# Expert weights in 8 KB rows: 128x2048 words a load, nineteen places, four column groups of one bank

## The chip, the cores and the metric

One Trainium2 chip, one of its cores. The metric is the device time of one execution in microseconds, as the median of several runs; a profile of one execution tells where that time goes. TensorE multiplies matrices into PSUM banks, VectorE (DVE), ScalarE (ACT) and GpSimd (POOL) work on tiles in SBUF and on those banks, and SyncE (SP) issues most DMAs. Sixteen DMA engines share the core's transfers.

## What is computed

The reference runs two blocks on one sequence of 256 tokens with 1024 features, all in float32. The first block has two layers of attention and a feed-forward net; the second has one token mixer (long convolution, a recurrence with states from a context) and a mixture of experts. The change is about that last part:

```python
def expert_choice_moe(h, p):
    cap = EC_CAPACITY * T // N_EXPERTS                  # 32 tokens an expert, 16 experts
    affinity = jax.nn.softmax((h @ p['router_w']).astype(jnp.float32), axis=-1)
    gates, idx = lax.top_k(jnp.swapaxes(affinity, 1, 2), cap)
    xe = jax.vmap(lambda hb, ib: hb[ib])(h, idx)
    hid = jax.nn.silu(jnp.einsum('becd,edf->becf', xe, p['exp_w1'])) * jnp.einsum('becd,edf->becf', xe, p['exp_w3'])
    ye = jnp.einsum('becf,efd->becd', hid, p['exp_w2']) * gates[..., None].astype(h.dtype)
    return jax.vmap(lambda ib, yb: jnp.zeros((T, D), yb.dtype).at[ib.reshape(-1)].add(yb.reshape(-1, D)))(idx, ye)
```

exp_w1 and exp_w3 are 1024 x 2048 for each expert and exp_w2 is 2048 x 1024: 24 MB of weights an expert, 16 of them.

## The kernel before

**Weights.** All weights but the experts' come through `Stream` (L64) in the order of their use, in loads of 1 MB into four tiles `wraw0` to `wraw3`, all on SyncE's queue. `pump_splits` (L94) splits pieces of 128x1024 words into two float32r parts: ACT casts into a tile `whi` (L113), DVE subtracts into a tile `wlo` (L114); there are three of each, and three pieces are split ahead. TensorE multiplies with both parts (`mm3`, L343). In most of these loads a row, which is what lies contiguously for one partition, is 1 or 2 KB long; the chunks of `modulation` (L371, from ada_w and mod_w) and the load of x into `xT` have rows of 8 KB, and the first eight of those chunks come in halves with rows of 4 KB.

**Slots.** Activations live in 26 equal tiles of 128x1024 words (`slot`, L311), three more from `tokens` (L1643) on. `drop` (L324) puts a slot at the end of the list of free ones and `slot` takes the first. A slot that is taken is a new tile of its tag, so its first writer waits for all users of the tile that had the tag before.

**The experts.** `Experts` (L149) lists the weights of the 16 experts in the order of their use as pieces of [128, 2, 512] words: 256 rows of 2 KB, 512 KB, 48 for each expert. Each goes into a room: at the start of `moe` (L1843) these are the free slots but five (`slot_rooms`, L1802), the halves of the stream's raw tiles and the six tiles whi and wlo (`stream_rooms`, L1812), then two halves of `xT` once its rows have been copied. `done` (L180) gives the room of the piece that was used last to the next load, or hands it back: the first five (`ex.back = 5`) become slots again. SyncE issues the loads (L1844) in this order; each waits for its room.

Before the first expert the router's product, the choice of 32 tokens for each expert and `pick` (L1897) must be done: one-hot products fetch the rows of four experts at a time into a tile `xe`, features on the partitions.

An expert then runs over four quarters `c` of its 2048 hidden features. For w1 and w3 it takes four pieces each; a piece holds two blocks of 128 input features, and block k0 + j is multiplied in column group (k0 + j) mod 4 of a bank, so a piece has two matmuls in two of the four groups of 32 columns. `part` (L1944) copies the bank, eight products with `i32` sum the four groups and turn them, ACT makes SiLU (L1952), DVE the product (L1953), and four pieces of w2 follow into two banks `py`. After the fourth quarter the sums `ye` (L1972) are multiplied with the gates and added to `acc` (L1991). After the last expert comes a norm, and four DMAs write the result (L2009).

The core of the inner loop:

```python
for k0 in range(0, 8, 2):
    w = ex.take()
    for j in range(2):
        q = 32 * (k0 % 4 + j)
        mm(p[q:q + 32, :], xe[e // 4][:, k0 + j, ee], w[:, j, :], start=k0 < 4, stop=k0 >= 4)
    ex.done()
```

All of TensorE's products are written on L340, so their tiles tell them apart: x<-s, x<-wraw and the like with 128x512 are w1 and w3, mm<-...,hid is w2, x<-i,part the turning. One float32 matmul is two instructions.

Of the kernel before, what the change touches and what calls it, by code (L numbers as in the profile page):

```python
# [27 lines left out]
NSLOT = 26  # L28
NLATE = 3
KEEP = 5  # L30
PICKS = ((0, 2), (1, 1), (2, 1))
SLOTW = 1024

# [5 lines left out]
class Slot:  # L39
    """A view of a slot's tile and the slot's tag."""  # L40

    def __init__(self, v, t, tag):
        self.v, self.t, self.tag = v, t, tag
# [5 lines left out]
class Halves:  # L49
    """Tiles that follow one another along the first free axis, `per` entries in each."""  # L50
# [13 lines left out]
class Stream:  # L64
    """The weights in the order of their use: chunks of 128 x 2048 words are loaded ahead. Pieces of a chunk are
    split ahead into two float32r parts whose sum is the weight, or stay as they are where the key is in `whole`; a
    chunk that comes with a function goes to it as it is, when the pieces before it have been taken."""
# [26 lines left out]
    def pump_splits(self):  # L94
        g = self.g
        nc = g.nc
        while self.split_pos < len(self.order) and self.split_pos < self.take_pos + self.ahead:
# [10 lines left out]
            hi = g.wsp.tile([128, 1024], FR, name="whi", tag="whi")  # L108
            lo = g.wsp.tile([128, 1024], FR, name="wlo", tag="wlo")
            hv = hi[:, :k * n].rearrange("p (k n) -> p k n", k=k)  # L110
            lv = lo[:, :k * n].rearrange("p (k n) -> p k n", k=k)
# [38 lines left out]
class Experts:  # L150
    """The experts' weights in the order of their use, [128, 2, 512] at a time, into whatever room there is."""

    def __init__(self, I, load):
        self.load = load
        self.aps = []
        for e in range(16):
            w1, w3, w2 = (I[n][0, e].rearrange("(k p) n -> p k n", p=128) for n in ("exp_w1_2", "exp_w3_2", "exp_w2_2"))
# [40 lines left out]
def constants():  # L198
# [7 lines left out]
    c["c_mask"] = np.ascontiguousarray(m.reshape(3, 2, 128, S).transpose(1, 2, 0, 3))  # L206

    # decay-ordered triangles within chunks of 64 tokens: rows s, columns t; per direction strict, inclusive
# [3 lines left out]
    # the implicit filter's features and decay window  # L212
# [8 lines left out]
    # real transforms over 512 points: cosines, sines (column 0: the alternating signs of the last frequency)  # L221
# [17 lines left out]
def vectors():  # L239
    """Vectors wanted one feature per partition: (name, input, its part, columns of 128)."""  # L240
# [12 lines left out]
def lay_out(inputs):  # L253
    """The inputs as the chip reads them: x and the context by features, the vectors side by side."""
# [38 lines left out]
def _build(g, I, out):  # L293
# [10 lines left out]
    more = []  # L304
    free_slots = [f"s{i}" for i in range(NSLOT)]

    def at(tag, shape, dt=FT):
        uid[0] += 1
        return (act if int(tag[1:]) < NSLOT else more[0]).tile(shape, dt, name=f"{tag}_{uid[0]}", tag=tag)

    def slot(name, shape, dt=FT):  # L311
# [4 lines left out]
        uid[0] += 1  # L316
        t = at(tag, [128, SLOTW], dt)
        v = t[:shape[0], :n]
# [3 lines left out]
        return Slot(v, t, tag)  # L322

    def drop(*ts):  # L324
        for t in ts:
            assert t.tag not in free_slots
            free_slots.append(t.tag)
# [3 lines left out]
    def wt(name, shape, dt=FT):  # L331
        """A short-lived tile, in the rotating slots of its size."""
# [19 lines left out]
    def by_tile(key, w, c0, c1):  # L352
        """Columns c0:c1 of a 1024-row matrix, out tile by out tile."""
# [17 lines left out]
    def modulation(m, i):  # L371
        """2048 columns of cond @ W, one feature per partition, into mods[m][:, 16 i:16 i + 16] (per vector)."""
# [35 lines left out]
    def among(main, asides):  # L408
        """The asides spread evenly over the main ones."""
# [62 lines left out]
    # vectors, one feature per partition  # L472
# [7 lines left out]
    # the first columns of the first layer's modulation, in slots  # L480
# [27 lines left out]
    # conditioning vectors, silu'd, as 32-column stationary operands with one (or two) live columns  # L508
# [17 lines left out]
    def reduce_angle(o, x, shape):  # L526
        """x less its nearest multiple of 2 pi."""
# [16 lines left out]
    def whole_gains(l):  # L544
        """The gains of the features that turn are in the tables."""
# [4 lines left out]
    def tables():  # L550
        """What the first layer's attention needs."""
# [33 lines left out]
        # lambda of both layers, on every partition  # L585
# [39 lines left out]
    def rsq(ss, scale, add):  # L625
        """(scale ss + add) ** -0.5 of a narrow tile."""
# [35 lines left out]
    def on_all(rs):  # L662
        """One number for each token, on every partition."""
# [7 lines left out]
    def rms_bcast(x):  # L671
        """(mean of squares over the features + eps) ** -0.5, on every partition."""
# [9 lines left out]
    def modulate(x, mul, add, exact=None, rs=None):  # L682
        """h = rms(x) * mul + add, split (and as it is)."""
# [22 lines left out]
    def wst(key, xh, xl, nk, tiles, finish, per=1, outer=False, bank="mm"):  # L706
        """Out tiles (128 features x 256 tokens), two to a bank; a piece holds `per` of them."""
# [26 lines left out]
    def alternate(gens):  # L734
        """Their steps in turn."""
# [8 lines left out]
    def staggered(gens, lag):  # L744
        """Their steps, each `lag` steps after the one before it; the later ones first."""
# [12 lines left out]
    def urgent(gen, n):  # L758
        """Its steps with a higher priority."""
# [11 lines left out]
    def layer(l):  # L771
# [85 lines left out]
        def attn_a(h, oh, ss, i0):  # L857
            """Head h: its output over the first component's sum of exponents, token by partition."""
# [45 lines left out]
        def heads_a(half):  # L904
# [3 lines left out]
            # the norm over a head's 128 features, features to the partitions  # L908
# [1123 lines left out]
```

## Time and profile before

| | us |
|---|---|
| median of 3 runs | 2614.85 |
| lowest, highest | 2611.32, 2617.59 |
| span of the profiled execution | 2612.7 |
| of it before the experts' steady transfers (0 to 1596) | 1596.0 |
| expert stage (1596 to 2598) | 1002.0 |
| end (2598 to 2612.7) | 14.7 |

For the profiled execution the span is the one time that is known; it lies 2.15 us under the median. In the profile PE is TensorE's matmuls and PEld its loads of stationary operands. The stretches are read from the views by windows and by time.

### The profile page before, as it was taken

The page shows a single profiled execution, that of the slowest core. Times are in us where ns is not written, and L with a number is a line of the kernel's source. Part 1 is how long each engine was busy: PE and PEld are TensorE (multiplying, and loading weights), DVE is VectorE, ACT ScalarE, POOL GpSimd, SP SyncE. Part 2 cuts the span into 40 slices and gives each one's busy share as a digit, 9 for nine tenths or more (in the row PEclk, how much of TensorE's full clock was granted, in tenths as well). Part 3 has the DMA queues.
Part 4 walks back from the last instruction along what each step waited for, and adds up shares of the span by engine and source line. Part 5 has one row for each costly group of instructions (what it writes and reads, how often), then busy time and mean ns, then how long its engine had stood idle before and what let it go on. Part 6 is the DMA issues. An engine that isn't in the chain of part 4 may idle for free. (4 is left out here: it accounts for less than half of the span.)

```text
span 2612.7 us, 39350 instructions
## 1 busy us (share of the span) xinstructions
PE 2364.9 (91%) x15946; PEld 1539.9 (59%) x15946; DVE 1179.6 (45%) x2239; ACT 833.8 (32%) x1539; POOL 114.0 (4%) x137
## 2 busy tenths in 40 slices
PE   7999999999999999998999888888888888888887
PEld 3678798898677777998987764332222222222222
DVE  5666577976667646667775552111111111111112
ACT  3654347545455423444562421110000000000001
POOL 0011000000011000000000010000000000000001
PEclk9999999999999998999999888899999999999999
DMA  9655554774655454655425376999999999999997
GB/s 352 217 181 193 171 180 167 226 244 156 244 190 197 158 189 133 200 181 170 145 84 158 98 246 213 386 386 387 386 387 387 387 386 386 386 386 386 384 386 284
DMA packets 386015, 678.35 MB, mean 260 GB/s; under 512 B 35208, under 2 KB 138153, under 8 KB 377514
## 3 DMA queue, kind: packets, MB, share of 16 engines
q1 hardware_dynamic: 384762, 671.64, 73.0%
q0 software_dynamic: 1072, 4.20, 0.4%
q8 instruction: 126, 2.06, 0.3%
q14 instruction: 55, 0.45, 0.0%
HBM read 671.31 MB, written 4.46 MB: 259 GB/s over the span
## 5 line engine op out<-in xcount | busy, mean ns | idle before, releaser
L340 PE MATMUL mm<-s,whi 128*128 128x256 f32 x3888 | 736.9, 289 | 12.0 <-DVE s L699 4.5
L340 PEld LDWEIGHTS mm<-s,whi 128*128 128x128 f32 x3888 | 614.8, 194 | 58.0 <-issue 33.2
L340 PE MATMUL mm<-s,wlo 128*128 128x256 f32 x1944 | 557.4, 287 | 2.2 <-DVE wlo L114 2.1
L340 PE MATMUL x<-s,s 128*32 128x512 f32 (+8 forms) x3276 | 462.7, 398 | 56.1 <-DMA s<-in_exp_w 51.8
L113 ACT CAST whi<-wraw 128x1024 fp32r<-128x1024 f32 x327 | 341.9, 1049 | 501.4 <-PE mm L340 408.0
L114 DVE TENSOR_TENSOR wlo<-wraw,whi 128x1024 fp32r<-128x1024 f32 x327 | 399.9, 1225 | 210.6 <-ACT whi L113 204.3
L340 PEld LDWEIGHTS mm<-s,wlo 128*128 128x128 f32 x1944 | 376.0, 194 | 14.0 <-issue 6.5
L1944 DVE COPY part<-x 128x512 f32<-128x512 f32 x64 | 44.3, 692 | 693.7 <-PE x L340 691.6
L340 PEld LDWEIGHTS x<-s,s 128*32 128x32 f32 (+5 forms) x3276 | 183.7, 141 | 287.4 <-DMA s<-in_exp_w 157.3
L340 PE MATMUL mm<-whi,s 128*128 128x512 f32 (+1 forms) x768 | 226.7, 373 | 2.1 <-ACT qn L818 1.5
L340 PEld LDWEIGHTS x<-i,part 128*128 128x128 f32 x1024 | 123.7, 191 | 149.6 <-DVE part L1944 92.6
L1944 ACT COPY part<-x 128x512 f32<-128x512 f32 x64 | 37.5, 585 | 460.4 <-PE x L340 460.4
L340 PE MATMUL x<-i,part 128*128 128x32 f32 x1024 | 137.1, 278 | 43.6 <-DVE part L1944 42.9
L340 PEld LDWEIGHTS mm<-whi,s 128*128 128x128 f32 x768 | 138.3, 190 | 40.2 <-issue 8.7
L340 PE MATMUL mm<-wlo,s 128*128 128x512 f32 (+1 forms) x384 | 143.7, 376 | 0.6 <-DVE wlo L114 0.6
L340 PE MATMUL mm<-s,hid 128*32 128x512 f32 x616 | 124.0, 739 | 21.0 <-DVE hid L1953 20.2
L1952 ACT ACTIVATE hid<-x 128x128 f32<-128x128 f32 x64 | 17.7, 277 | 389.9 <-PE x L340 389.9
L630 POOL TENSOR_TENSOR ry<-ru,nhalf 128x8 f32<-128x8 f32 (+4 forms) x47 | 73.0, 1555 | 865.1 <-DVE ru L629 648.9
L340 PE MATMUL x<-wraw,s 128*32 128x512 f32 x352 | 84.1, 616 | 13.0 <-DMA wraw<-in_exp_w 13.0
L340 PE MATMUL g<-wraw,cond 128*32 128x512 f32 x512 | 90.1, 621 | 4.2 <-DMA wraw<-in_ada_w 2.5
L340 PEld LDWEIGHTS mm<-wlo,s 128*128 128x128 f32 x384 | 73.0, 190 | 23.9 <-issue 4.1
L340 PEld LDWEIGHTS mm<-s,hid 128*32 128x32 f32 x616 | 27.0, 121 | 74.3 <-DVE hid L1953 25.8
(389 smaller groups left out, 2264.2 us busy)
## 6 DMA issues: line engine op xcount, KB each, us to landing
s<-in_exp_w SPq DMA_DIRECT2D x460, 512.0 KB, 10.8
wraw<-in_w_in SPq DMA_DIRECT2D x83, 1024.0 KB, 5.4
wraw<-in_exp_w SPq DMA_DIRECT2D x132, 512.0 KB, 10.8
wraw<-in_ada_w SPq DMA_DIRECT2D x40, 1024.0 KB, 5.0
whi<-in_exp_w SPq DMA_DIRECT2D x66, 512.0 KB, 10.8
wlo<-in_exp_w SPq DMA_DIRECT2D x66, 512.0 KB, 10.8
wraw<-in_w_mlp_up SPq DMA_DIRECT2D x32, 1024.0 KB, 5.5
wraw<-in_w_mlp_down SPq DMA_DIRECT2D x32, 1024.0 KB, 5.1
```

What stands on the lines that cost most here:

```text
L113: nc.scalar.copy(hv, src)
L114: nc.vector.tensor_sub(lv, src, hv.bitcast(FT))
L340: nc.tensor.matmul(*a, **k)
L630: nc.gpsimd.tensor_tensor(y, u, nhalf[:sh[0]].to_broadcast(sh), op=OP.pow)
L1944: (nc.vector.tensor_copy if i else nc.scalar.copy)(t, p)
L1952: nc.scalar.activation(hid, p[:, 0:128], AF.Silu)
```

## The change

- An expert's weights come in rows of 8 KB: 128x2048 words, 1 MB a load. For w1 and w3 a load is one block of 128 input features with all 2048 hidden ones; for w2 a row holds two neighbouring hidden features' 1024 words. There are 24 loads an expert, 384 in all.
- The places for them are 128x2048: `whi` and `wlo` become one tile `whl` of two halves, the raw tiles are used whole, `xT` is one place, and the slots become halves of 13 tiles (`Pair`), with one pair and one single tile more from `tokens` on. 12 pairs, 3 raw tiles, 3 `whl` and `xT` make nineteen places; two are handed back (`ex.back = 2`).
- `slot` takes the half that was freed longest ago, of a pair in use if no more than four pairs are wholly free (and of the same type of number), else of any. A pair that is wholly free begins a new tile. `gate` takes the newest (`newest=True`) where the list was turned round.
- `hidden` multiplies a load in four matmuls, one for each 512 hidden features, in the four column groups of one bank, over eight loads. Two such banks (w1, w3) are copied and turned by transposes with every second column, SiLU and product run over 512 columns, and the eight loads of w2 go into one bank `py`, 64 rows for each half of the features. The copy of `py`, the gates' products over 64 rows and the sums follow.
- `pick` runs after experts 0, 1 and 4; the fourth set of rows reuses the first's tile. The last norm's gains are made at the start of expert 15.
- The mask of the second attention is one tile of four parts and one DMA, not two tiles of three parts and two DMAs.

```diff
@@ Stream.pump_splits
-            hi = g.wsp.tile([128, 1024], FR, name="whi", tag="whi")
-            lo = g.wsp.tile([128, 1024], FR, name="wlo", tag="wlo")
+            hl = g.wsp.tile([128, 2, 1024], FR, name="whl", tag="whl")
+            hv, lv = (hl[:, j, :k * n].rearrange("p (k n) -> p k n", k=k) for j in range(2))
@@ Experts
-            for c in range(4):
-                self.aps += [w[:, k:k + 2, 512 * c:512 * c + 512] for w in (w1, w3) for k in range(0, 8, 2)]
-                self.aps += [w2[:, k:k + 2, a:a + 512] for k in (4 * c, 4 * c + 2) for a in (0, 512)]
+            for n in ("exp_w1_2", "exp_w3_2"):
+                w = I[n][0, e].rearrange("(k p) n -> k p n", p=128)
+                self.aps += [w[k] for k in range(8)]
+            w = I["exp_w2_2"][0, e].rearrange("(m p j) n -> m p (j n)", p=128, j=2)
+            self.aps += [w[m] for m in range(8)]
@@ slot
-        tag = free_slots.pop(0)
+        free = [(q.freed[h] if q.used else max(q.freed), i, h) for i, q in enumerate(pairs) for h in range(q.width)
+                if h not in q.used and (not q.used or q.dt == dt)]
+        halves = [f for f in free if pairs[f[1]].used]
+        _, i, h = (max if newest else min)(halves if halves and sum(not q.used for q in pairs) <= SPARE else free)
+        q = pairs[i]
+        if not q.used:
+            q.new(dt)
@@ layer
-        maskt = [slot("maskc", [128, 3, S]) for _ in range(2)]
-        for t in range(2):
-            nc.gpsimd.dma_start(maskt[t].v, I["c_mask"][t])
+        maskt = slot("maskc", [128, 4, S])
+        nc.gpsimd.dma_start(maskt.v, I["c_mask"])
@@ stream_rooms
-        return [half(t, i) for t in raw for i in range(2)] + [room("whi"), room("wlo")] * 3
+        return [room(g.wraw, r) for r in ws.rooms] + [room(g.wsp, "whl")] * 3
@@ moe
-        ex.more(slot_rooms(KEEP))
+        whole = sorted((q for q in pairs if q.width == 2), key=lambda q: max(q.freed))
+        ex.more(slot_rooms(whole[:-2]))
...
-        ex.back = 5
+        ex.back = 2
+        def hidden():
+            p = pst("mm")
+            for k in range(KT):
+                w = ex.take()
+                for c in range(4):
+                    mm(p[32 * c:32 * c + 32, :], x_[:, k, ee], w[:, 512 * c:512 * c + 512], start=k == 0, stop=k == KT - 1)
+                ex.done()
+            return p
...
+            for i, src in enumerate((pa, pb)):
+                t = wt("part", [128, 512])
+                (nc.vector.tensor_copy if i else nc.scalar.copy)(t, src)
+                p = pst("x")
+                for b in range(4):
+                    a = 256 * (b // 2) + b % 2
+                    nc.tensor.transpose(p[:, 128 * b:128 * b + 128], t[:, a:a + 255:2], ident)
+                hid.append(p)
+            h = wt("hid", [128, 512])
+            nc.scalar.activation(h, hid[0], AF.Silu)
+            nc.vector.tensor_tensor(h, h, hid[1], op=OP.mult)
+            py = pst("mm")
+            for m in range(8):
+                w = ex.take()
+                for j in range(2):
+                    a = 128 * (2 * (m % 2) + j) + 32 * (m // 2)
+                    for i in range(2):
+                        q = 64 * i + 32 * j
+                        mm(py[q:q + 32, :], h[:, a:a + 32], w[:, 1024 * j + 512 * i:1024 * j + 512 * i + 512],
+                           start=m == 0, stop=m == 7)
+                ex.done()
```

## Rows read from the trace of the kernel before

**Rows 1.** Page: DMA's busy tenths and rate in 40 slices of the span.

```profile
DMA  9655554774655454655425376999999999999997
GB/s 352 217 181 193 171 180 167 226 244 156 244 190 197 158 189 133 200 181 170 145 84 158 98 246 213 386 386 387 386 387 387 387 386 386 386 386 386 384 386 284
```

**Rows 2.** Chain of waits, 1300 to 2620 us: shares by line.

```profile
by line: DMA s<-in_exp_w 32.8%; PE x L340 17.0%; DMA wraw<-in_exp_w 11.5%; PE mm L340 7.6%; DMA whi<-in_exp_w 5.7%; DMA xT<-in_exp_w 4.2%; DVE part L1944 1.6%; issue 1.3%; DMA wlo<-in_exp_w 0.8%; DVE hid L1953 0.6%; ACT hid L1952 0.6%; POOL
```

**Rows 3.** Windows by stretch (first line names the columns).

```profile
core 0: us, PE busy (x) PEld busy (x) DVE busy (x) ACT busy (x) POOL busy (x), PEclk, DMA share, GB/s
0.00:1596.00 1596.00, 1523.44 (x11606) 1259.27 (x11607) 1050.09 (x1991) 750.60 (x1352) 107.19 (x131) 0.96 0.55 184
1596.00:2598.00 1002.00, 837.64 (x4336) 279.24 (x4331) 120.61 (x235) 80.19 (x179) 0.00 (x0) 0.95 1.04 383
```

**Rows 4.** Timeline (start, length, instruction, idle before): one waiting load; then data in place.

```profile
2045.37 0.14 PEld L340 LDWEIGHTS x<-wraw,s 128*32 128x32 f32 x4 [1.21 <-DMA wraw<-in_exp_w]
2045.37 1.05 PE L340 MATMUL x<-wraw,s 128*32 128x512 f32 x4 [0.30 <-DMA wraw<-in_exp_w]
...
1637.44 3.64 PE L340 MATMUL x<-s,s 128*32 128x512 f32 x32
```

**Rows 5.** Expert loads issued before 1596 (tile view), and the page's issue-to-landing time.

```profile
L1844 SPq DMA_DIRECT2D s<-in_exp_w x24: 367/368/1441, 1469.5 to 1554.2; - x24
...
L1844 SPq DMA_DIRECT2D xT<-in_exp_w x2: 368/368/368, 1574.6 to 1575.1; - x2
...
s<-in_exp_w SPq DMA_DIRECT2D x460, 512.0 KB, 10.8
```

**Rows 6.** Timeline: the first refill, and TensorE at the last landing.

```profile
1596.38 9.81 SPq L1844 DMA_DIRECT2D s<-in_exp_w  x11
...
2597.10 0.14 PEld L340 LDWEIGHTS mm<-s,hid 128*32 128x32 f32 x4 [0.57 <-DMA s<-in_exp_w]
```

**Rows 7.** DMA packets in 57:58, 51:53, 12:14, 46.6:48, 49:50 and 1700:2500; one window.

```profile
DMA packets 53, 0.43 MB, mean 434 GB/s; under 512 B 0, under 2 KB 0, under 8 KB 0
DMA packets 120, 0.87 MB, mean 437 GB/s; under 512 B 8, under 2 KB 8, under 8 KB 15
DMA packets 128, 0.86 MB, mean 428 GB/s; under 512 B 12, under 2 KB 12, under 8 KB 35
DMA packets 70, 0.57 MB, mean 410 GB/s; under 512 B 0, under 2 KB 0, under 8 KB 0
DMA packets 200, 0.41 MB, mean 410 GB/s; under 512 B 0, under 2 KB 0, under 8 KB 200
DMA packets 160021, 308.93 MB, mean 386 GB/s; under 512 B 9412, under 2 KB 9412, under 8 KB 159983
...
59.00:60.00 1.00, 1.00 (x6) 0.82 (x5) 1.00 (x3) 0.00 (x0) 0.47 (x1) 1.00 1.04 389
```

**Rows 8.** An expert's small steps: copy, gate transposes, gate products (tile view, timeline).

```profile
L1944 DVE COPY part<-x x56: 691/692/693, 1641.2 to 2527.4; 128x512 f32<-128x512 f32 x56
...
2071.12 0.41 PE L1978 MATMUL x<-ident,gd 128*128 128x128 f32 x2
2074.76 3.71 PE L340 MATMUL x<-ye,gT 128*128 128x512 f32 x8
```

**Rows 9.** SyncE's waits for TensorE, 1400 to 2612 (us, times, longest).

```profile
SPq L1844 <- PE x L340: 106.8, 136, 20.9
```

**Rows 10.** Windows of 10 us around the routing (columns as in rows 3).

```profile
1560.00:1570.00 10.00, 5.98 (x41) 3.56 (x40) 5.01 (x11) 3.21 (x6) 1.97 (x2) 0.55 0.27 101
1570.00:1580.00 10.00, 4.14 (x21) 3.81 (x21) 7.99 (x30) 2.57 (x5) 0.00 (x0) 0.67 0.32 105
1580.00:1590.00 10.00, 9.10 (x27) 4.80 (x28) 3.56 (x11) 0.91 (x2) 3.04 (x8) 0.58 0.01 2
```

**Rows 11.** TensorE's and ACT's waits before 1596 (us, times, longest).

```profile
PE mm L340 <- DVE s L699: 4.5, 2, 3.5
...
ACT whi L113 <- PE mm L340: 408.0, 209, 9.2
```

More of the change, by code (lines that the diff above doesn't have):

```diff
@@ L302, in const, with __init__, new, slot @@
         return pool.tile(shape, dt, name=name, tag=name)
[L304 to L311, printed above, removed]
+    class Pair:
+        def __init__(self, tag, pool, width=2):
+            self.tag, self.pool, self.width = tag, pool, width
+            self.used, self.freed, self.tile, self.dt = set(), [0] * width, None, None
+        def new(self, dt=FT):
+            uid[0] += 1
+            self.tile = self.pool.tile([128, self.width * SLOTW], dt, name=f"{self.tag}_{uid[0]}", tag=self.tag)
+            self.dt = dt
+            return self.tile
+    pairs = [Pair(f"s{i}", act) for i in range(NPAIR)]
+    clock = [0]
+    def slot(name, shape, dt=FT, newest=False):
         n = int(np.prod(shape[1:]))
         assert n <= SLOTW, (name, shape)
-        tag = free_slots.pop(0)
-        uid[0] += 1
-        t = at(tag, [128, SLOTW], dt)
-        v = t[:shape[0], :n]
+        free = [(q.freed[h] if q.used else max(q.freed), i, h) for i, q in enumerate(pairs) for h in range(q.width)
[5 more added lines that the diff above has]
+            q.new(dt)
+        q.used.add(h)
+        v = q.tile[:shape[0], SLOTW * h:SLOTW * h + n]
         if len(shape) > 2:
@@ L1643, in tokens @@
         def tokens():
-            more.append(g.late())
-            free_slots.extend(f"s{NSLOT + i}" for i in range(NLATE))
+            pool = g.late()
+            for w in (2, 1):
+                pairs.append(Pair(f"s{len(pairs)}", pool, w))
+                pairs[-1].freed = [clock[0] + 1] * w
             nc.vector.scalar_tensor_tensor(pre[:, 2], m2(4, 0), 1.0, col["norm2_pre"], op0=OP.add, op1=OP.mult)
@@ L1714, in tokens @@
                 n += 1
-            free_slots[:] = free_slots[-2:] + free_slots[:-2]
-            gt.parts = [slot("gate", [128, 4, S]) for _ in range(2)]
+            gt.parts = [slot("gate", [128, 4, S], newest=True) for _ in range(2)]
             with tc.high_priority(0):
@@ L1800, in second, with slot_rooms, room, back @@
         return ctx_proj, ctx_states, hyena_filter, tokens
-    def slot_rooms(keep=0):
-        def room(tag):
-            return lambda: at(tag, [128, 2, 512]), lambda: free_slots.append(tag)
-        r = [room(free_slots.pop(0)) for _ in range(len(free_slots) - keep)]
-        return r
-    def half(t, i):
-        return (lambda: t[:, 1024 * i:1024 * i + 1024].rearrange("p (k n) -> p k n", k=2)), lambda: None
+    def slot_rooms(whole):
+        def room(q):
+            q.used = {0, 1}
+            def back():
+                clock[0] += 1
+                q.used, q.freed = set(), [clock[0]] * 2
+            return q.new, back
+        return [room(q) for q in whole]
     def stream_rooms():
-        def room(tag):
-            return (lambda: g.wsp.tile([128, 1024], FT, name=tag, tag=tag).rearrange("p (k n) -> p k n", k=2)), lambda: None
-        raw = [g.wraw.tile([128, 2048], FT, name=r, tag=r) for r in ws.rooms]
-        return [half(t, i) for t in raw for i in range(2)] + [room("whi"), room("wlo")] * 3
+        def room(pool, tag):
+            return lambda: pool.tile([128, 2048], FT, name=tag, tag=tag), lambda: None
+        return [room(g.wraw, r) for r in ws.rooms] + [room(g.wsp, "whl")] * 3
     def routing():
@@ L1844, in moe @@
         ex = Experts(I, lambda t, ap: nc.sync.dma_start(t, ap))
-        ex.more(slot_rooms(KEEP))
+        assert not any(q.used for q in pairs)
+        whole = sorted((q for q in pairs if q.width == 2), key=lambda q: max(q.freed))
+        ex.more(slot_rooms(whole[:-2]))
         ex.more(stream_rooms())
+        go = slot("go", [128, 2, 512])
         ss = squares(xT)
@@ L1879, in moe @@
                     lambda n: xT[:, n, 128 * t:128 * t + 128], 8)
-        ex.more([half(xT.rearrange("p k t -> p (k t)"), i) for i in range(2)])
+        ex.more([(lambda: xT.rearrange("p k t -> p (k t)"), lambda: None)])
         m8 = wt("m8", [16, 8])
@@ new lines, in hidden @@
+        def hidden():
[6 more added lines that the diff above has]
+            return p
+        for e in range(16):
+            es_, ee, x_ = slice(32 * e, 32 * e + 32), slice(32 * (e % 4), 32 * (e % 4) + 32), xe[e // 4]
+            if e == 15:
+                drop(oh)
+                gb = slot("gb", [128, D])
+                for k4 in (0, 4):
+                    p = pst("x")
+                    for k in range(4):
+                        b = wt("gcol", [128, 128])
+                        nc.vector.tensor_copy(b, pre[:, 4, k4 + k:k4 + k + 1].to_broadcast([128, 128]))
+                        mm(p[:, 128 * k:128 * k + 128], b, ident, start=True, stop=True)
+                    nc.scalar.copy(gb[:, 128 * k4:128 * k4 + 512], p)
+            if e == 0:
+                pa, pb = hidden(), hidden()
+                acc = [slot("moe", [128, D]) for _ in range(2)]
+            else:
+                pa, pb = hidden(), hidden()
+            hid = []
+            for i, src in enumerate((pa, pb)):
+                t = wt("part", [128, 512])
+                (nc.vector.tensor_copy if i else nc.scalar.copy)(t, src)
+                p = pst("x")
+                for b in range(4):
[10 more added lines that the diff above has]
+                    a = 128 * (2 * (m % 2) + j) + 32 * (m // 2)
+                    for i in range(2):
+                        q = 64 * i + 32 * j
+                        mm(py[q:q + 32, :], h[:, a:a + 32], w[:, 1024 * j + 512 * i:1024 * j + 512 * i + 512],
+                           start=m == 0, stop=m == 7)
+                ex.done()
+            if e in PICKS:
+                if len(xe) < 3:
+                    xe.append(slot("xe", [128, KT, 128]))
+                else:
+                    xe.append(xe[0])
+                pick(len(xe) - 1)
+            ty = wt("ye", [128, 512])
+            nc.scalar.copy(ty, py)
@@ L1980, in moe, with part @@
             nc.scalar.copy(gT, p[:, :S])
+            def part(t, i):
+                p = pst("x")
+                mm(p, gT[64 * i:64 * i + 64, 128 * t:128 * t + 128], ty[64 * i:64 * i + 64], start=True, stop=True)
+                return p
             if e == 15:
```

95 lines of the change are left out of this document (21 added, 74 removed).

## The prediction

> **What bounds the kernel now.** I read the page's slices first [rows 1]. Their last row splits the span in two: in slices 2 to 25 the transfers run at 84 to 246 GB/s, after them at 384 to 387 with the DMA engines full, up to the last. That second stretch is the expert stage, which streams 16 experts' weights. The chain of waits over it is made of waits for DMA of expert weights: s, wraw, whi, xT and wlo add up to 55% of that window [rows 2]. By stretches [rows 3] the first 1596 us hold 1523.4 us of TensorE work (1596.0 - 1523.4 = 72.6 idle, 184 GB/s), the expert stage 1002 us with TensorE "busy" 837.6 but 383 GB/s. Its busy time is misleading, and the timeline shows why: each load brings two matmuls (four instructions), they take 1.05 us, and the weight load before them has waited 1.21 us for a DMA [rows 4]. The same kind of matmul with data in place and four column groups filled goes 32 instructions in 3.64 us, which is 0.91 us per four matmuls, or 0.455 us per load. So TensorE could eat a load in less than half the 1.36 us that one takes. The stage is bound by the transfer rate of 2 KB rows; the first 1596 us are bound by TensorE.
>
> **The change, part by part.**
>
> Rate of the loads. 16 experts x 24 MB are 768 loads of 512 KB now, and 384 of 1 MB after. Before the stage 38 are issued (five rows of destinations, 24 + 6 + 3 + 3 + 2 = 38; first and last shown) [rows 5]; after, 12 pairs, 3 wraw, 3 whl and xT give 19 places, the same 19 MB. So 730 loads remain before, 365 after. The first of them is issued at 1596.38 and the last has landed at 2597.10 [rows 6]: 1000.7 us. At 386 GB/s, steady over 800 us [rows 7], one load takes 524288 / 386e9 = 1.358 us, 730 take 991.6, and 9.1 us are start-up, which I keep.
>
> What do 8 KB rows run at? The kernel has some: x and the chunks of ada_w come in 8 KB rows. A microsecond at 57 holds 53 packets, none under 8 KB, at 434 GB/s; so such a row does go as one packet. Two stretches that are mostly such packets give 437 and 428. One at 46.6 gives 410, all in 8 KB packets. A microsecond of 2 KB rows amid them gives 410, another 389, on average 400, and sustained they give 386, 0.97 of it [rows 7]. I take 425: the mean of 434, 437, 428 and 410 is 427, and between that and 0.97 x 427 = 415 it lies nearer to the three saturated rows. Ends: 410 and 437. One 1 MB load then takes 1048576 / 425e9 = 2.467 us (2.557 and 2.399), 365 take 900.5, with start-up 909.6 (942.4 and 884.7). **Gain 91.1 us (58 to 116).**
>
> [...]
>
> Does TensorE keep up? Per expert after: 24 loads x 0.91 = 21.8; eight transposes and two of the gates at 0.41 a pair, 2.1; four products with the gates 3.7 at most (half the rows now); and where the hidden layer is made, waits of a DVE copy (0.69), SiLU and product over 512 columns (no row of that size; bounded by half and twice the 512-column copy, 0.35 to 1.4 each, I take 0.69, the copy's own) and the copy of py, 0.69: 2.8 [rows 4, 8]. Sum 30.4 us against 24 x 2.467 = 59.2 of DMA. All of it lies beside the transfers; the py bank, the fewer copies (128x512 twice an expert, not eight times) and the fewer small matmuls gain nothing for the same reason. The reserve: eight loads are in flight (10.8 us to landing [rows 5] / 1.358), so after the two places given back 17 - 8 = 9 places of 2.467 = 22 us let TensorE lag, against 26 x 1.358 = 35 now. The longest lag is about the 9 us outside the products; it fits.
>
> Start of the steady stream. SyncE waits up to 20.9 us [rows 9] because the first five rooms eaten (now two, the same megabytes) aren't refilled. The refill now needs six loads, that is all eight features of the picked rows; after, the third load needs three of them. DMA stands nearly still meanwhile, 2 GB/s from 1580 to 1590 [rows 10]. Ends 0 and 16 us (1596.4 - 1580, the start of that window); I take **5 us gain**: three of six loads are left out, but the picked rows come one by one, not at once.
>
> Whole pairs must be free before an early load starts, and those loads stand in SyncE's queue ahead of the last w_out chunks and of the DMA of expert 0; with 1 MB in each of eight places a chunk issued behind them waits 20 us, not 11. The early loads have slack from 1575 to 1596. At worst nothing lands before 1560: then 384 x 2.467 = 947 us from there on, 2507, against 1596.4 - 5 + 909.6 = 2501 for the last landing. Cost 0 to 6.
>
> The first 1596 us. Slots are now halves of 13 tiles, reused in another order, and a pair that begins anew waits for both halves' readers; hi and lo are one tile. The trace can't show these waits; nearest is the wait for a slot's writer that TensorE has today (4.5 us in two waits, 3.5 the longest); ACT's casts wait 408 us for TensorE, so they run ahead and whl costs nothing [rows 11]. Bounds: -5 (those gone) and +20 (six waits of 3.5). With the queue above I take **3 us loss**. The mask in one DMA of 512 KB, not two of 384, lies beside the gate's products: 0. Tail: the last MB brings four matmuls (1.05, as now), one copy instead of two in parallel: **1 us loss** (0 to 5).
>
> Sum: 2612.7 - 91.1 - 5 + 3 + 1 = 2520.6. The profiled execution spans 2612.7; the median of the three runs is 2614.85, 2.1 more, so **2523**.
>
> **Rivals.**
> 1. Longer rows run no faster in a sustained stream (something behind the packets limits it at 386). For: the stage sits at 384 to 387 for 900 us. Against: 434 and 437, if short [rows 7]. Time: 2614.9 - 5 + 4 = 2614, no change.
> 2. Only a third is gained: a cost per packet that is small beside its bytes. By 400 GB/s (below the lowest 8 KB row, 410) a load takes 2.621, 365 + start-up 965.9, gain 34.8, time 2579. [...] The rows of 410 to 437 speak against it.
> 3. TensorE becomes the bound at its lower clock. [...] Against: a TensorE that is late is busy without a break, and over the stage, busy 84% of it, the clock is 0.95 [rows 3]. [...]
> 4. Slower: the pairs cost the TensorE-bound part. Place: the first 1596 us, the attention and recurrence stages, which take and drop slots all the time. Price: every wait for a neighbour half adds its length. It decides when the idle time there grows by over 92 us, from 72.6 to 165 or more, some 30 waits of 3.5 us. With 35 such waits, 2523 + 122 = 2645. Against: TensorE waits 4.5 us for slots now, and old slots were also equal and reused.
>
> **How the numbers follow.** Forecast 0.78, rival 1 0.04, rival 2 0.07, rival 3 0.07, rival 4 0.04. Forecast's own range: 2523 - 25 - 5 - 7 = 2486 to 2523 + 33 + 20 = 2576 if all ends met at once; they rarely do, and 2498 to 2562 takes in the ends of the rate by itself (2498, 2556) and rival 3. Rivals 1, 2 and 4 (0.15) are left out. Some 0.2% (5 us) is what a measurement can tell from no change: faster 0.92 (forecast, rivals 2 and 3), same 0.04 (rival 1), slower 0.04 (rival 4).
>
> **What would show it.** In the profile after: a rate of 415 to 435 GB/s flat over the expert stage, about 20 us from issue to landing of a load, and the chain of waits still on DMA of expert weights. TensorE's busy time in the stage should fall to around half, and four matmuls follow each landing. Steady transfers should begin between 1585 and 1597, with the first stretch within 1590 to 1616. I am wrong if the rate is under 405, if DMA shows gaps while SyncE waits for TensorE, or if the experts start 20 us later.

## The result, and the profile after

The kernel after takes **2531.76 us** (median of 4 runs, 2525.54 to 2536.05), the kernel before beside it 2615.46 (4 runs): ratio 0.9675, 95% interval 0.9656 to 0.9694. Five more runs later gave 2532.12, ratio 0.9683 (0.9670 to 0.9697). That is 82 to 84 us less where 92 were forecast. The profiled execution after spans 2534.3 us, its time is 2536.05, the longest of the four.

The page of the kernel after: DMA's busy tenths and rate in 40 slices, and the queue's issues with KB each and us from issue to landing.

```profile
DMA  9555454674655546355442616899999999999996
GB/s 353 207 190 200 158 192 156 203 247 145 228 204 200 192 165 216 124 179 183 149 138 84 182 68 249 322 421 421 421 421 421 421 421 421 421 422 421 421 421 284
...
s<-in_exp_w SPq DMA_DIRECT2D x230, 1024.0 KB, 19.8
```

Where [rows 1] had 386 the stage now runs flat at 421. The DMA view of 1700 to 2450 of after says what the rows are: as many packets under 8 KB as under 512 bytes, so none of the weights' packets is shorter than 8 KB.

```profile
DMA packets 43356, 315.93 MB, mean 421 GB/s; under 512 B 4814, under 2 KB 4814, under 8 KB 4814
```

Windows of after (us, busy time of PE, PEld, DVE, ACT, POOL with instructions, granted clock, DMA share, GB/s), against [rows 3]:

```profile
0.00:1596.00 1596.00, 1520.98 (x11566) 1262.08 (x11570) 1052.47 (x1990) 748.72 (x1349) 104.56 (x129) 0.96 0.55 184
1640.00:2500.00 860.00, 566.42 (x3082) 113.69 (x3082) 63.26 (x116) 34.80 (x67) 0.00 (x0) 0.76 1.01 421
```

The stage is still the DMA's: its chain of waits (1300 to 2540) is made of the same places as [rows 2], with 72% of the window where there were 55.

```profile
by line: DMA s<-in_exp_w 43.4%; DMA wraw<-in_exp_w 14.4%; PE mm L358 10.0%; DMA whl<-in_exp_w 9.7%; PE x L358 7.5%; DMA xT<-in_exp_w 4.8%; PE g L358 2.4%; issue 1.2%; PE x L1120 0.5%; POOL ry L648 0.4%; DVE whl L111 0.4%; DMA s<-in_rw_g_up 
```

**Where the time went.** The timelines of after give four marks: the load into xT, the first refill, the last landing, the end.

```profile
1585.59 0.33 SPq L1862 DMA_DIRECT2D xT<-in_exp_w  x1
1598.55 3.41 SPq L1862 DMA_DIRECT2D s<-in_exp_w  x2
...
2515.70 0.20 PEld L358 LDWEIGHTS mm<-s,hid 128*32 128x32 f32 x8 [2.26 <-DMA s<-in_exp_w]
```

Against [rows 5, 6] the spans differ as follows:

| stretch | before | after | difference | forecast |
|---|---|---|---|---|
| start to the load into xT | 1574.6 | 1585.6 | +11.0 | +3 |
| from there to the first refill | 21.8 | 13.0 | -8.8 | -5 |
| first refill to last landing | 1000.7 | 917.2 | -83.6 | -91.1 |
| last landing to the end | 15.6 | 18.6 | +3.0 | +1 |
| sum | 2612.7 | 2534.3 | -78.4 | -92.1 |

### The profile page after: what moved, and what is told of

Its sections match the earlier page's. It is cut to its first block, busy times and chain, and to the rows that moved or that the text cites. A ratio compares the mean times of both kernels' runs of the same rounds, so it can differ in the third digit from the quotient of the medians.

```text
span 2534.3 us, 36197 instructions
## 1 busy us (share of the span) xinstructions
PE 2143.7 (85%) x15050; PEld 1394.5 (55%) x15050; DVE 1127.4 (44%) x2127; ACT 797.2 (31%) x1443; POOL 110.5 (4%) x135
## 3 DMA queue, kind: packets, MB, share of 16 engines
q0 software_dynamic: 1040, 3.67, 0.4%
q8 instruction: 118, 1.93, 0.3%
## 4 chain that ended last, share of the span: by engine, by line
DMA 36%; PE 12%; DVE 2%; issue 1%; POOL 0%; ACT 0%; SPq 0%; DVEq 0%; POOLq 0%; ACTq 0%
DMA s<-in_exp_w 21%; DMA wraw<-in_exp_w 7%; PE mm L358 7%; DMA whl<-in_exp_w 5%; PE x L358 4%; DMA xT<-in_exp_w 2%; PE g L358 1%; PE x L1120 0%; POOL ry L648 0%; DVE whl L111 0%; DMA s<-in_rw_g_up 0%; POOL s L2032 0%; DVE s L695 0%; DVE s L2038 0%; DVE s L1492 0%
## 5 line engine op out<-in xcount | busy, mean ns | idle before, releaser
L358 PE MATMUL mm<-s,whl 128*128 128x256 f32 x5832 | 763.1, 289 | 15.0 <-DVE s L717 4.5
L358 PEld LDWEIGHTS mm<-s,whl 128*128 128x128 f32 x5832 | 724.5, 194 | 72.7 <-issue 35.1
L110 ACT CAST whl<-wraw 128x1024 fp32r<-128x1024 f32 x327 | 341.9, 1049 | 503.5 <-PE mm L358 425.1
L111 DVE TENSOR_TENSOR whl<-wraw,whl 128x1024 fp32r<-128x1024 f32 x327 | 399.9, 1225 | 212.2 <-ACT whl L110 210.2
L358 PE MATMUL mm<-whl,s 128*128 128x512 f32 (+2 forms) x1504 | 314.7, 466 | 41.0 <-DMA whl<-in_exp_w 38.5
L358 PE MATMUL mm<-s,s 128*32 128x512 f32 (+1 forms) x1232 | 216.1, 792 | 94.9 <-DMA s<-in_exp_w 93.6
L358 PEld LDWEIGHTS mm<-whl,s 128*128 128x128 f32 (+1 forms) x1504 | 202.7, 174 | 146.0 <-DMA whl<-in_exp_w 80.4
L358 PE MATMUL x<-s,s 128*64 128x64 f32 (+8 forms) x1924 | 179.5, 272 | 7.4 <-DVE s L1299 1.9
L358 PEld LDWEIGHTS x<-s,s 128*64 128x64 f32 (+4 forms) x1924 | 130.4, 159 | 53.8 <-issue 28.0
L648 POOL TENSOR_TENSOR ry<-ru,nhalf 128x8 f32<-128x8 f32 (+4 forms) x47 | 71.2, 1519 | 1004.1 <-DVE ru L647 643.3
L358 PEld LDWEIGHTS mm<-s,hid 128*32 128x32 f32 x616 | 14.7, 122 | 126.9 <-DMA s<-in_exp_w 115.4
L358 PE MATMUL mm<-wraw,s 128*32 128x512 f32 x360 | 59.7, 757 | 27.3 <-DMA wraw<-in_exp_w 27.3
```

The source lines that it names most:

```text
L110: nc.scalar.copy(hv, src)
L111: nc.vector.tensor_sub(lv, src, hv.bitcast(FT))
L358: nc.tensor.matmul(*a, **k)
L648: nc.gpsimd.tensor_tensor(y, u, nhalf[:sh[0]].to_broadcast(sh), op=OP.pow)
```

## The experiments

Theory: in the stage only the length of a row counts, through a cost of each packet. Rivals: the larger loads, the fewer matmuls and waits, or the place in the queue bring the gain; TensorE or the number of places limits what is left. Beside that, the first stretch and the ends had to be priced. Each time is a median, with the ratio to the kernel before on the same chip.

**e1_rows2k: the change with 2 KB rows in its 1 MB loads.**

```diff
-                w = I[n][0, e].rearrange("(k p) n -> k p n", p=128)
-                self.aps += [w[k] for k in range(8)]
+                w = I[n][0, e].rearrange("(k p) n -> p k n", p=128)
+                self.aps += [w[:, k:k + 4, 512 * c:512 * c + 512] for k in (0, 4) for c in range(4)]
```

(w2 likewise, `w[:, k:k + 4, 512 * c:512 * c + 512]`.)

> The changed kernel with its 1 MB loads, places and products, but each load gathers rows of 2 KB (1 KB of words from each of four row blocks), so the products pair the wrong blocks and the experts' part of the result is not the reference's. Theory (the length of a row sets the rate): the stream falls back to 386 GB/s, 1048576 / 386e9 = 2.716 us a load against 2.491 at the 421 GB/s of the changed kernel, 365 x 0.225 = 82 us more: 2614 us (2605 to 2622). Rival (half as many DMAs, or four column groups a load, made the gain): 421 GB/s stays and so does the time, 2532.

Measured: 2614.98 us (8 runs), ratio 0.9991 (0.9976 to 1.0006). The whole gain is gone, with the size of the loads, the places and the number of products as in the change. Its DMA view of the same window:

```profile
DMA packets 145826, 289.94 MB, mean 387 GB/s; under 512 B 4416, under 2 KB 4416, under 8 KB 145801
```

**e2_rows4k: the change with 4 KB rows.**

```diff
-                self.aps += [w[k] for k in range(8)]
+                self.aps += [w[:, k:k + 2, 1024 * c:1024 * c + 1024] for k in range(0, 8, 2) for c in range(2)]
...
-            self.aps += [w[m] for m in range(8)]
+            self.aps += [w[:, k:k + 2] for k in range(0, 16, 2)]
```

> The changed kernel with 1 MB loads of rows of 4 KB (two row blocks a load; products pair the wrong blocks, so the experts' part of the result is not the reference's). Theory (each packet costs a fixed time plus its bytes): an engine takes 84.9 ns a 2 KB packet (16 of them in 1.358 us) and 311 ns an 8 KB one (8 in 2.491), so 9.4 ns plus 37.7 ns a KB; a 4 KB packet takes 160, 16 of them 2.566 us, 409 GB/s, 365 x 0.075 = 27 us more: 2559 us (2553 to 2565). Rival (a limit on the whole stream near 421 that 4 KB rows reach too): 2532. Rival (only rows of 8 KB help): 2614.

Measured: 2558.9 us (2 runs), ratio 0.9780 (0.9757 to 0.9803), 409 GB/s:

```profile
GB/s 409 409 409 409 409 410 408 410 409 410 408 410 409 409 409 410 409 409 409 410 409 409 408 409 409 409 410 410 408 408 410 409 410 409 409 409 410 409 409 408
DMA packets 79516, 306.85 MB, mean 409 GB/s; under 512 B 4674, under 2 KB 4674, under 8 KB 79489
```

**e3_before_rows4k: the kernel before, its 512 KB loads in 4 KB rows.** The places, the products and the order of the code stay.

```diff
-                self.aps += [w[:, k:k + 2, 512 * c:512 * c + 512] for w in (w1, w3) for k in range(0, 8, 2)]
-                self.aps += [w2[:, k:k + 2, a:a + 512] for k in (4 * c, 4 * c + 2) for a in (0, 512)]
+                self.aps += [w[:, k, a:a + 1024] for w in (w1, w3) for k in (2 * c, 2 * c + 1) for a in (0, 1024)]
+                self.aps += [w2[:, k] for k in range(4 * c, 4 * c + 4)]
```

> The kernel before with its 512 KB loads, rooms, slots and products, but a load is 128 rows of 4 KB instead of 256 of 2 KB; the products pair the wrong blocks, so the experts' part of the result is not the reference's. Theory (fixed time a packet): 8 x 160 ns = 1.283 us a load against 1.358, 730 x 0.075 = 55 us less: 2560 us (2553 to 2567), 409 GB/s. Rival (the 1 MB load is what counts): 386 GB/s and 2615.

Measured: 2563.69 us (2 runs), ratio 0.9799 (0.9771 to 0.9826), 409 GB/s:

```profile
DMA packets 84093, 306.59 MB, mean 409 GB/s; under 512 B 9340, under 2 KB 9340, under 8 KB 84055
```

The rate is the same for loads of 512 KB and of 1 MB, for 38 places of 512 KB and 19 of 1 MB, for two matmuls a load and four. In these runs it goes by the length of a row alone: 386 or 387, 409, 421 for 2, 4 and 8 KB. A last rival is that the rows of a load must lie back to back in memory, as those of the change do. The 4 KB rows speak against it: in e2_rows4k w2's loads are whole rows of the matrix, back to back, those of w1 and w3 are halves of 8 KB rows; an expert takes about 62 us, and none of the 40 slices of 18.75 us above leaves 408 to 410.

**e5_twice: every matmul of an expert's loads twice.**

```diff
-                for c in range(4):
-                    mm(p[32 * c:32 * c + 32, :], x_[:, k, ee], w[:, 512 * c:512 * c + 512], start=k == 0, stop=k == KT - 1)
+                for r in range(2):
+                    for c in range(4):
+                        mm(p[32 * c:32 * c + 32, :], x_[:, k, ee], w[:, 512 * c:512 * c + 512], start=k + r == 0,
+                           stop=k + r == KT)
```

(The four of a load of w2 likewise.)

> The changed kernel with every product of the experts' weights made twice, so that the experts' sums are not the reference's. [...] Theory (the transfers bound the stage, and a busier TensorE is granted the higher clock): 24 x 1.9 + 9 = 55 us of work an expert under 59.8 of DMA, the same time within 0.3%, 2526 to 2538, with the granted clock of the stage up from 0.76 to 0.9 or more. Rival (TensorE at the clock of 0.76 is near its limit): it becomes the bound, 24 x 2.5 + 11 = 71 us an expert, 16 x 11 = 180 us more, 2710.

Measured: 2537.18 us (2 runs), ratio 0.9704 (0.9685 to 0.9723). Its window of the stage:

```profile
1640.00:2490.00 850.00, 717.63 (x5940) 200.05 (x5936) 62.23 (x116) 40.65 (x77) 0.00 (x0) 1.00 1.01 421
```

SyncE's wait for TensorE from 1600 to 2510 (us, times, longest), first of this kernel, then of after:

```profile
SPq L1862 <- PE mm L358: 69.1, 52, 5.5
```

```profile
SPq L1862 <- PE mm L358: 11.1, 20, 2.7
```

With nearly twice the instructions TensorE's granted clock went from 0.76 to 1.00, the rate stayed at 421. A load's 16 instructions, 1.9 us in the expected sum, take 1.92 at that clock. So a TensorE twice as loaded still is not the bound. The 5 us over the change (2531.76, 2532.12) are as many as the first refill lost, 17.8 us after the load into xT and not 13.0; from there to the last copy it lost 4.6 more, and at the start and the end of its profiled execution it gained.

**e6_13places: the change without the six places in wraw and whl.**

```diff
-        ex.more(stream_rooms())
```

> The changed kernel without the six places in the stream's tiles: 13 places. Theory (a place is worth only what it loads before the first expert; eight loads in flight and three places of reserve, 7.5 us, hide TensorE's lag at the end of an expert): 6 x 2.49 = 15 us more, 2541 to 2552, DMA still at 421 GB/s without gaps. Rival (the reserve is too small, a lag of about 9 us stops the transfers 1.5 us or more in each expert): 39 us or more on top of 2532, 2571 and up.

Measured: 2546.6 us (2 runs), ratio 0.9740 (0.9720 to 0.9759), still 421 GB/s, and SyncE waits for TensorE 8.8 us in all. So 13 places keep the stream full too; what the six places are worth is that their 6 MB are fetched ahead of the stage: 14.5 us, 2.4 a place, near one load's 2.49.

**e4_pairs_only: the pairs, whl and the mask, with the experts' loads as before** (2 KB rows, 512 KB, four rooms handed back). Cut to the core; `Pair`, `slot` and the mask are those of the change.

```diff
-NSLOT = 26
-NLATE = 3
-KEEP = 5
-PICKS = ((0, 2), (1, 1), (2, 1))
+NPAIR = 13
+PICKS = ((0, 2), (1, 1), (4, 1))
+SPARE = 4
...
-        ex.back = 5
+        ex.back = 4
```

> The slots as halves of 13 tiles, hi and lo in one tile and the one mask of the changed kernel, with the experts' 512 KB loads of 2 KB rows and their products as before, in the halves of the same places (38 of them). Theory A (pairs and whl cost the first 1596 us what the changed kernel lost there, 11 us by the time of the load into xT): that load is issued at about 1585 instead of 1574.6 and the time is 2622 to 2628. Theory B (the 11 us come from the order in which the experts' 1 MB loads and the last weights share SyncE's queue, or from chance): the load is issued at 1572 to 1578 and the time is 2612 to 2618.

Measured: 2617.11 us (10 runs), ratio 1.0004 (0.9990 to 1.0018). In its profiled execution the load into xT is issued at 1582.4 (1574.6 before), the first refill 16.1 us behind it (21.8 before): a loss and a gain that cancel. The load comes nearly as theory A has it, the time is theory B's. Four rooms are 2 MB, what the change hands back. The next kernel undoes that one number.

**e10_pairs_back5: the same with five rooms handed back, as before.**

```diff
-        ex.back = 4
+        ex.back = 5
```

> The pairs, whl and the mask as in the change, the experts' loads in 2 KB rows as before, and the first refill called after the sixth room as before. Theory, the pairs cost some 6 us of the stretch before the experts and the fourth room's call gave them back in the kernel with the pairs alone: load into xT at about 1581 us, first refill 21 to 22 us behind it, 2621 us (2618 to 2625). Rival, the pairs cost nothing and the profiled executions only scattered: 2615 us, load into xT at 1575.

Measured: 2622.08 us (7 runs), ratio 1.0025 (1.0014 to 1.0037), first refill 21.7 us behind the load into xT. So the new slots, whl, the mask and what goes with them (the later third `pick`) cost some 6 us (3.7 to 9.7), and the earlier refill gives 5.6 back.

**e11_whl_only: the kernel before with whi and wlo as halves of one tile.**

```diff
-            hi = g.wsp.tile([128, 1024], FR, name="whi", tag="whi")
-            lo = g.wsp.tile([128, 1024], FR, name="wlo", tag="wlo")
+            hl = g.wsp.tile([128, 2, 1024], FR, name="whl", tag="whl")
```

> The kernel before with whi and wlo as two halves of one tile whl, and nothing else changed. Theory, whl costs nothing since both halves were allocated together anyway: 2615 us (2612 to 2618), load into xT at 1574.5. Rival, the later release of the two halves carries the 6 us: 2621 us, load into xT at 1581.

Measured: 2618.49 us (11 runs), ratio 1.0012 (1.0003 to 1.0021): 0.8 to 5.5 us, between the two expectations. No wait was found that carries it: ACT's casts, which run ahead, wait 419.1 us for TensorE (408.0 in [rows 11]) and once 1.3 us for DVE's use of whl. Where its profiled execution loses 3 us against before is between 1020 and 1075, where both blocks meet. Windows there, first before, then e11_whl_only:

```profile
1020.00:1030.00 10.00, 9.01 (x19) 4.36 (x18) 7.89 (x14) 2.18 (x4) 0.00 (x0) 0.50 0.00 0
1030.00:1040.00 10.00, 10.00 (x68) 10.00 (x67) 7.38 (x12) 2.19 (x4) 0.00 (x0) 0.73 0.01 2
```

```profile
1020.00:1030.00 10.00, 9.06 (x16) 3.69 (x14) 6.84 (x12) 2.19 (x4) 0.00 (x0) 0.50 0.00 0
1030.00:1040.00 10.00, 9.96 (x46) 9.96 (x47) 8.43 (x14) 2.19 (x4) 0.00 (x0) 0.50 0.01 2
```

From 1030 to 1040 TensorE is busy 10.00 and 9.96 us; before, the granted clock is up to 0.73 and 68 matmuls are done, in e11_whl_only it stays at 0.50 and 46 are done. Why it rises later, and whether whl has a part in it or this one execution by chance, is not shown.

**e7_spare0: the change with `SPARE = 0`**, so that of all free halves the one freed longest ago is taken.

```diff
-SPARE = 4
+SPARE = 0
```

> The change, but a pair's second half is taken only where it is the one that has been free longest (the spare count of 4 is 0). Theory, the pairs' order of reuse holds early loads back: load into xT nearer to 1575 than to 1582 and 2526 us. Rival, the order of reuse is of no account: 2532 us, load into xT at 1579 to 1586.

Measured: 2534.05 us (4 runs), ratio 0.9691 (0.9678 to 0.9704). Another order of reuse does not bring the 6 us back.

**e8_late_back and e12_spare0_late: an earlier first refill, a shorter end.** The first two rooms are refilled and the next two handed back; the last additions are written so that none waits behind the other tile's final one, and the second tile's products with the gains run on DVE, not on POOL. The diff is cut to its core. e12 has `SPARE = 0` besides.

```diff
-        ex.back = 2
...
-                pa, pb = hidden(), hidden()
+                pa = hidden()
+                ex.back = 2
+                pb = hidden()
...
-                nc.gpsimd.tensor_tensor(o, o, gb[:, 512 * i:512 * i + 512], op=OP.mult)
+                if t == 0:
+                    nc.gpsimd.tensor_tensor(o, o, gb[:, 512 * i:512 * i + 512], op=OP.mult)
+        for i in range(2):
+            o = acc[1][:, 512 * i:512 * i + 512]
+            nc.vector.tensor_tensor(o, o, gb[:, 512 * i:512 * i + 512], op=OP.mult)
...
+        for t in range(2):
             for i in range(2):
                 c = slice(512 * i, 512 * i + 512)
-                nc.vector.scalar_tensor_tensor(xo[t][:, c], acc[t][:, c], rs, xo[t][:, c], op0=OP.mult, op1=OP.add)
+                nc.vector.scalar_tensor_tensor(xo[t][:, c], acc[t][:, c], rss[t], xo[t][:, c], op0=OP.mult, op1=OP.add)
```

> The changed kernel with two small moves: the first two rooms go to new loads, and the two that become slots again are those of loads 9 and 10; after the last expert all four sums come first, and two of the four products with the gains run on DVE instead of POOL. Theory (the stage ends one stream after its first refill, and the tail after the last landing is a chain of small steps): the first refill comes 3 to 5 us earlier against the load into xT (13.0 us before it now, 8 to 10 then) and the tail takes 4 us less than 18.6, so 7 to 9 us less than the changed kernel on the same chip. Rival (other waits end the stage, the rooms are missed later): 0 to 2 us less.

> The change with the spare count at 0, the first refill called after the second room, and the last additions put so that none waits behind the other tile's final one. If both gains hold and add up: 2523 us (2520 to 2527). If only the refill and the tail gain: 2529.6 us. If neither holds: 2532 us.

Measured: 2529.62 (4 runs), ratio 0.9677 (0.9661 to 0.9693), and 2531.64 (4 runs), ratio 0.9679 (0.9666 to 0.9692). In both profiled executions the two terms are there, 1.7 us at the refill and 2.3 at the end, 4.0 together where 7 to 9 were expected; the medians can't tell these kernels from the change (2531.76, 2532.12). No version clearly beats it.

**e9_after_again: the change unchanged**, for the scatter.

> The changed kernel once more, for a closer median. Theory (what the profiled execution lost in its first 1596 us, 11 us, is the granted clock of that execution and not the slots): the median of many runs lies at 2526 to 2532, and a second profile has the load into xT at another time than 1585.6, anywhere from 1571 to 1586. Rival (the pairs cost it in each execution): the load comes at 1584 to 1587 again and the median is 2531 to 2536.

Measured: 2532.12 us (5 runs), at the border of the two expectations; the load into xT, at 1581.5, is in the first one's range and outside the second's. The profiled executions side by side (the end here counts from the last copy into `ye`):

| kernel | load into xT | refill, behind it | refill to last copy | end | median |
|---|---|---|---|---|---|
| before | 1574.6 | 21.8 | 1001.8 | 14.5 | 2614.85 |
| after | 1585.6 | 13.0 | 918.9 | 16.9 | 2531.76 |
| e9_after_again | 1581.5 | 13.0 | 919.0 | 16.9 | 2532.12 |
| e1_rows2k | 1570.9 | 12.8 | 999.5 | 16.9 | 2614.98 |
| e2_rows4k | 1584.2 | 12.4 | 945.1 | 16.9 | 2558.90 |
| e3_before_rows4k | 1574.5 | 21.8 | 947.1 | 15.0 | 2563.69 |
| e4_pairs_only | 1582.4 | 16.1 | 1004.1 | 14.5 | 2617.11 |
| e5_twice | 1579.7 | 17.8 | 923.5 | 15.0 | 2537.18 |
| e6_13places | 1578.3 | 12.8 | 934.3 | 17.8 | 2546.60 |
| e10_pairs_back5 | 1577.5 | 21.7 | 1002.9 | 15.5 | 2622.08 |
| e11_whl_only | 1577.7 | 21.9 | 1002.3 | 14.6 | 2618.49 |
| e7_spare0 | 1582.6 | 13.0 | 918.8 | 16.8 | 2534.05 |
| e8_late_back | 1586.7 | 11.3 | 920.4 | 14.6 | 2529.62 |
| e12_spare0_late | 1580.7 | 11.3 | 918.8 | 14.6 | 2531.64 |

For like loads the last three spans repeat to a microsecond or two; the first one moves by 16 us among kernels with the same slots (1570.9 to 1586.7). For it, medians of many runs are the evidence, one profile is not.

## Why the prediction was right, step by step

2531.8 lies 8.8 above the 2523 of the forecast and in its range. The mechanism was right; four sizes were off.

- **Rate.** 425 was taken, 421 came. 365 x (1048576 / 421e9 = 2.491) = 909.1, plus 8.0 of start-up, gives the 917.2; the forecast had 909.6. This is the largest term that was mis-sized, 7.6 us, and the reason lies in the rows chosen: the windows of [rows 7] that were leant on hold one or two microseconds. Such a window counts whole packets, and in 1 us one packet of 8 KB more or less is 8 GB/s. In the sustained stream of after, 40 windows of 1 us (1800 to 1801, 1813 to 1814 and so on) read 393 to 459 GB/s, 421 on average; two of them, 1865 to 1866 and 1917 to 1918:

```profile
DMA packets 63, 0.46 MB, mean 459 GB/s; under 512 B 7, under 2 KB 7, under 8 KB 7
DMA packets 52, 0.39 MB, mean 393 GB/s; under 512 B 4, under 2 KB 4, under 8 KB 4
```

  So 434, 437, 428 and 410 are all readings that a stream of 421 gives. The scale of 0.97 had no better ground: 40 such windows in the stage of before read 379 to 391, 386 on average, so a short window does not stand above its own stream, and one of the two leant on, 410, is above all of these. That 421 lies halfway between the scaled figure (415, 414 when worked out) and the mean of 427 is luck.
- **First refill.** -8.8 instead of -5. e4_pairs_only and e10_pairs_back5 show 5.6 of it as what handing back 2 MB instead of 2.5 gives; e1_rows2k has 12.8 us with short rows, so the rest comes with the larger loads and the order of their products, and not from their rate.
- **First stretch.** +3 was taken out of -5 to +20. By medians the pairs, whl and mask cost 5.9 (e10_pairs_back5 over the 2616.18 beside it). Most of that seems to be lost early: at the border of the blocks SyncE issues the first load of w_mlp_down at 1011.4 and 1012.7 in the profiles of e3_before_rows4k and before, at 1013.5 in e11_whl_only, and at 1013.7 to 1019.3, 1016.5 on average, in the eleven with pairs. The +11 of the profiled execution holds more than that. How much of it is the clock is not shown: before too has a stretch at 0.50 (1440 to 1460). But executions with the same slots differ in it. In the recurrence the granted clock was 0.52 in this execution from 1455 to 1465, where a product x<-x,s of 64x64 takes 316 ns (223 ns from 1475 to 1485, at 1.00), and 1.00 in that of e1_rows2k, which reaches the load into xT 14.7 us earlier. Windows of after, then of e1_rows2k:

```profile
1455.00:1465.00 10.00, 9.27 (x103) 8.28 (x104) 4.88 (x12) 3.80 (x12) 0.00 (x0) 0.52 0.01 2
1485.00:1495.00 10.00, 9.97 (x104) 8.82 (x103) 4.79 (x12) 3.73 (x10) 0.00 (x0) 0.56 0.00 0
```

```profile
1455.00:1465.00 10.00, 9.11 (x182) 7.79 (x182) 6.18 (x16) 6.56 (x18) 0.00 (x0) 1.00 0.01 2
1485.00:1495.00 10.00, 8.61 (x206) 7.71 (x203) 7.35 (x18) 1.65 (x5) 0.00 (x0) 1.00 0.51 177
```

  "whl costs nothing" is not borne out as it was put: e11_whl_only is 0.8 to 5.5 us slower, though not, as far as found, through the waits of ACT that the prediction looked at. What carries the rest of the 5.9 stays open: an order of reuse nearer to the old one gains nothing (e7_spare0), the mask and the pairs themselves were not taken apart. The steady transfers began at 1598.6, just behind the 1585 to 1597 that were named (1594.5 in e9_after_again).
- **Tail.** +3.0 instead of +1. The prediction saw the single copy of py; it missed DVE's order. Timeline of after: the second tile's last addition (L2029) stands behind the first tile's final one (L2038), which waits for POOL.

```profile
2523.77 2.40 DVE L2038 SCALAR_TENSOR_TENSOR s<-s,ry,s 128x512 f32<-128x512 f32 x2 [0.97 <-POOL ry L648]
...
2526.10 0.67 DVE L2029 TENSOR_TENSOR s<-s,x 128x512 f32<-128x512 f32 x1
```

  With the additions reordered and two products moved to DVE (e8_late_back, e12_spare0_late) the end is 2.3 us shorter. The order is most of it: in e5_twice these lines are as in the change and all four products stay on POOL, but DVE did all four additions before the first final one, and the end is 15.0 us, 1.9 shorter than in after. (POOL's operands in all its rows here are tiles in SBUF; the banks are read by DVE and ACT.)
- **TensorE keeps up:** right, with more room than was worked out. SiLU over 512 columns took 0.60 us and the product 0.69, where 0.69 was taken for each. The reserve of nine places was not needed: 13 places do (e6_13places). But "busy around half" was wrong: 566.4 of 860 us is 66%; the granted clock fell to 0.76, and at 0.50 a load's products take 1.93 us instead of 1.06 (below).

**The rivals.** Rival 1 (no faster) falls with 421 against 387 in e1_rows2k, which differs in its rows alone. Rival 2 (400 GB/s) falls with 83.6 us from the first refill to the last landing, where it had 34.8; 4 KB rows alone gave 409. The cost of a packet that it names came out at 3.1% of an 8 KB packet's own time (last section). Rival 3 was half right: the granted clock did fall, from 0.95 to 0.76 over the stage. The timeline of after shows why it costs nothing:

```profile
2105.05 1.06 PE L358 MATMUL mm<-whl,s 128*32 128x512 f32 x8 [1.42 <-DMA whl<-in_exp_w]
2107.53 1.94 PE L358 MATMUL mm<-whl,s 128*32 128x512 f32 x8 [1.42 <-DMA whl<-in_exp_w]
2110.01 1.93 PE L358 MATMUL mm<-whl,s 128*32 128x512 f32 x8 [0.54 <-DMA whl<-in_exp_w]
```

A load's four matmuls take 1.06 us at a granted clock of 1.00 (2105.0 to 2106.2) and 1.93 at 0.50 (2110 to 2112), and a load comes every 2.48. Nor did a fuller TensorE stay at the lower clock: in e5_twice, busy 717.6 of 850 us, it had 1.00. Rival 4 needed 92 us more idle time in the first 1596 us; it rose from 72.6 to 75.0.

**Sums of the prediction.** The ends that it names (rate, refill, first stretch, tail) add up to 2478 and 2582 us if all are met at once, not to 2486 and 2576. Its range of 2498 to 2562 did not rest on them. No run shows the term that the range takes in as rival 3, a stage bound by TensorE at a lower clock: at 0.76 the rate was 421 GB/s.

## What to carry to other kernels

Where the DMA engines are full, lay weights so that a row, what one partition reads in one piece, is as long as the tile allows: from 2 to 8 KB the same bytes came 9% faster (387 to 421 GB/s), and neither larger loads nor fewer instructions had a part in it. Rows longer than 8 KB were not measured. Take the rate of such a stream from a sustained stretch; where only short windows are at hand, take many of them: single ones of 1 us were up to 38 GB/s off here. In a stage bound by transfers TensorE's granted clock may fall, here to 0.76 on average; compare a load's matmuls at the lowest clock seen (1.93 us at 0.50) with the time between two loads (2.48) before you fear it.

## What the runs showed of the hardware

- **A packet's time is nearly linear in its length from 2 to 8 KB.** Sixteen engines at 386 GB/s take 2048 x 16 / 386e9 = 84.9 ns for 2 KB, at 421 GB/s 311.3 ns for 8 KB: 9.4 ns and 37.7 ns a KB, so that at 8 KB the fixed part is 9.4 / 301.9 = 3.1% of the bytes' own time (9.1 ns and 3.0% with the 387 of e1_rows2k). That gives 160.3 ns or 409 GB/s for 4 KB, which e2_rows4k and e3_before_rows4k then showed.
- **The granted clock scatters between executions of one kernel, and in some kernels the time with it.** The four runs of after took 2525.5, 2529.0, 2534.5 and 2536.1 us at mean clocks of 0.896, 0.898, 0.889 and 0.889; the two shortest of e1_rows2k (2601.9, 2605.0) have 0.854 and 0.853, its two longest (2618.0, 2618.5) 0.843. Not every kernel shows it: of 17 runs of before on one chip the shortest (2612.0) has 0.955 and the longest (2619.3) 0.954.
- **More work gave a higher clock:** with the products doubled (e5_twice) the stage ran at 1.00 instead of 0.76.
